# Hybrid mixer layers: gate and up blocks moved among the branch blocks, planner durations and buffer pools changed

## The chip, the core and the metric

The kernel runs on one core of a Trainium2 chip. The metric is the device time of one execution in microseconds; the median of three runs is quoted. "Layer" below is one of the two layers of the model that the kernel computes in one launch.

## What is computed

The input x is one sequence of 256 tokens by 2048 columns. Each of two layers does the following (all in float32):

```
h      = rmsnorm(x)
proj   = h @ w_in                      # 2048 columns in, 35 blocks of columns out
ya     = dilated_window_attention(a_q, a_k, a_v; three groups of four heads) * silu(a_z)
yb     = latent_attention(b_cq, b_ckv, b_kr) * silu(b_z)
yc     = mlstm(c_qk, c_v, c_i, c_f, c_o) * silu(c_z)
yd     = state_space_scan(d_u) with a small gated linear layer * silu(d_z)
up[n]  = y[n] @ w_up[n]                # n = a, b, c, d: 512 -> 2048
merged = sum over n of sigmoid(gate[n] + merge_b[n]) * up[n]
x      = x + merged @ w_out
```

## The kernel before

**Weights.** Every float32 weight is streamed from HBM once, in units of 512 KB (two k-tiles of 128 rows by 512 columns). `Stream.split` (lines 322 to 338) splits each unit into a high part `wh` (ScalarE, a cast) and a low part `wl` (VectorE, a subtraction of two SBUF operands). `Stream.get` (line 340) keeps up to three units split ahead of TensorE and six issued ahead on the queue of SyncE. `block` (line 385) multiplies one block: for each k-tile and each of the two token halves it issues three matmuls of 128x128 by 512 columns (high by high, high by low, low by high). A projection block ("in") of 512 columns has 16 k-tiles, so 96 matmuls and 8 units. An up block has 4 k-tiles, 24 matmuls and 2 units. An output block has 96 again.

**Order of the blocks.** `layer_sequence` (line 265) writes the order out by hand. First come 19 head blocks (cqkr, du, x, cqk, bz, cv, co, cz, aq0, ak0, av0, aq1, ak1, av1, az, aq2, ak2, av2, dz) with four small blocks of branch b between them. Then come the 16 gate blocks, named g + column quarter d (0 to 3) + branch n (0 to 3 for a, b, c, d), with d outside and n in the order b, c, a, d. From the sixth gate on, each gate block is followed by the up block of the gate five places before (`LAG = 5`). The small block "glu" of branch d stands after the fifth gate (`GLU_AT = 4`). Four output blocks o0 to o3 end the layer.

**What a gate and an up block leave for other engines.** The gate block's evacuation is two VectorE operations from PSUM into the tile `gate`, then one tanh on ScalarE. The bias row `mb` is loaded by a DMA on the queue of SyncE at the block's start, into a tile that has one buffer. `merge` (line 1332) follows an up block: two VectorE operations per block, and for all but the first branch of a quarter one GpSimd addition into the accumulator `macc`. The last branch of a quarter spawns `merged` (line 1347), which transposes and splits the sum for the output blocks.

**Branches.** The four branches are Python generators, emitted in small steps between the units of the blocks. Branch d has 16 scan steps of four VectorE products and scans, four GpSimd products and sums (`enter`, `scan`, `leave`, lines 1172 to 1210) with the tables of `d_table` (line 1096); its matmuls are called `dbu` and `dyp`. Branch a (`a_group`, line 676, and `softmax_pv`, line 613) has three groups; its matmuls are `sc`, `pt` and `pv`, and its transposes `tt` and `yt`.

**The planner.** All engine calls go through `Eng` (line 162), whose call stands on line 198; so nearly every instruction shows line 198, and tiles must be read instead. At build time `Plan` (line 107) keeps a clock for each engine from a formula per operation. `tick` (line 364) is called after each unit and emits branch steps in the order e, q, m, b, c, a, d:

```
def can(self, need):
    now = self.clk["PE"] - self.SLACK
    if any(self.ready.get(a.name, (0.0, 0))[0] > now for a in need):
        return False
...
def free(self):
    lim = self.clk["PE"] + self.BACK
    return max(self.clk[e] for e in ("DVE", "ACT", "POOL")) <= lim
...
if not plan.free():
    return
if chains.get(n) and plan.can(need.get(n, ())) and step(n):
```

BACK is 2600 ns. Where a block needs a result that has not been emitted, the rest of that branch is emitted at once: `until("d", ...)` before glu, and `until("abcd"[n], ...)` before an up block. Every engine runs its instructions in the order of emission.

**Pools.** Tiles of 128x1024 come from one pool of `S4B = 28` buffers, tiles of 128x512 from one of `H2B = 12`. A new tile's first writer waits for the last reader of the tile whose buffer it takes; the planner does not know of these waits.

Of the kernel before, what the change touches and what calls it, by code (L numbers as in the profile page):

```python
# [35 lines left out]
LAG = 5  # L36
S4B, H2B, WARM = 28, 12, 8
GLU_AT = 4
# [23 lines left out]
for _d in range(4):  # L62
    for _n in UP_ORDER:
        COLS.append((f"g{_d}{_n}", _rng(GATE + _n * D + _d * 512)))
# [42 lines left out]
class Plan:  # L107
    """Estimates when each engine gets through what has been emitted so far, to choose what to emit next."""
# [4 lines left out]
    def __init__(self, nc):  # L113
        self.nc = nc
        self.clk = dict(PE=0.0, ACT=0.0, DVE=0.0, POOL=0.0, DMA=0.0)
        self.ready, self.used = {}, {}
        self.banks, self.pins = [], set()
        self.sine = False

    LAT = dict(PE=60.0, ACT=140.0, DVE=130.0, POOL=100.0, DMA=100.0)  # L120

    def run(self, eng, cost, outs, ins):
        t = self.clk[eng]
        for a in list(ins) + list(outs):
            r, e = self.ready.get(a, (0.0, eng))
            if e != "PE" or eng != "PE":
                t = max(t, r + self.LAT[e])
        for a in outs:
            u, e = self.used.get(a, (0.0, eng))
            if e != eng:  # L130
                t = max(t, u + self.LAT[e])
        t += cost
        self.clk[eng] = t
        for a in list(outs) + list(ins):
            self.used[a] = (max(t, self.used.get(a, (0.0, eng))[0]), eng)
        for a in outs:
            self.ready[a] = (t, eng)

    def bank(self, tile):
        """The branch bank that a new tile takes: free ones first, then the one that is free soonest."""  # L140
        if len(self.banks) < 4:
            self.banks.append(tile.name)
            return
        free = [b for b in self.banks if b not in self.pins]
        old = min(free, key=lambda b: self.used.get(b, (0.0, 0))[0])
        self.banks[self.banks.index(old)] = tile.name
        self.used[tile.name] = self.used.get(old, (0.0, "PE"))

    def can(self, need):
        """Whether the tensor engine could go on with these tiles and two banks without waiting."""  # L150
        now = self.clk["PE"] - self.SLACK
        if any(self.ready.get(a.name, (0.0, 0))[0] > now for a in need):
            return False
        return 4 - len(self.banks) + sum(b not in self.pins and self.used.get(b, (0.0, 0))[0] <= now
                                         for b in self.banks) >= 2
# [6 lines left out]
class Eng:  # L162
# [3 lines left out]
    def __getattr__(self, name):  # L166
        fn = getattr(self._r, name)
        p, e = self._p, self._e

        def call(*args, **kw):  # L170
            aps = [(k, a) for k, a in list(enumerate(args)) + list(kw.items()) if isinstance(a, bass.AP)]
            outs = [a for k, a in aps if k in (0, "out", "accum_out")]
            ins = [a for k, a in aps if k not in (0, "out", "accum_out")]
            n = max(a.free_size() if callable(a.free_size) else a.free_size for a in (outs if name != "reduce_sum"
                    and name != "reduce_max" else ins))
            psum = any(a.space == bass.MemoryType.PSUM for _, a in aps)
            srcs = [a.space == bass.MemoryType.PSUM for k, a in aps if k not in (0, "out", "accum_out")]
            ptr = any(k in ("scale", "bias", "scalar", "scalar1", "scalar2") or e == "DVE" and isinstance(k, int)
                      and name != "tensor_tensor" and a.free_size() == 1 for k, a in aps)
            if e == "PE":  # L180
                cost = 108.0 if name == "transpose" else 2.3 + (n if kw["lhsT"].dtype == F32R else 4 * max(n, P)) / 2.4
                if aps[0][1].shape[0] <= 32:
                    cost = 122.0 if name == "matmul" else 108.0
            elif e == "ACT":
                cost = 0.833 * n + (52 if any(srcs) else 92) + 93 * (ptr + ("accum_out" in kw))
                f = kw.get("func", args[2] if len(args) > 2 else None)
                if f in (AF.Sin, AF.Exp, AF.Tanh) and (f == AF.Sin) != p.sine:
                    p.sine = not p.sine
                    cost += 1283
            elif e == "POOL":  # L190
                cost = 160 + 0.84 * n if name == "tensor_scalar" else 145 + 2.11 * n
            elif name == "reciprocal":
                cost = 68 + 6.1 * n
            else:
                cost = 68 + n * (0.52 if name in ("tensor_scalar", "tensor_copy", "memset") and not psum else 1.04)
                cost += 62 * ptr
            p.run(e, cost, [a.name for a in outs], [a.name for a in ins])
            return fn(*args, **kw)  # L198

        return call  # L200
# [3 lines left out]
def hybrid_kernel(ctx: ExitStack, tc: tile.TileContext, x_in, pos, win, wup, wout, wuq, wukv, wglu, pp_in, db_in,  # L204
# [60 lines left out]
    def layer_sequence(l):  # L265
        seq = []
        for nm, _ in COLS:
            if nm[0] == "g":
                break
            seq.append(("in", nm))  # L270
            if nm in SMALL:
                seq.append(SMALL[nm])
        gs = [nm for nm, _ in COLS if nm[0] == "g"]
        for i, nm in enumerate(gs):
            seq.append(("in", nm))
            if i == GLU_AT:
                seq.append(("glu", "glu"))
            if i >= LAG:
                seq.append(("up", gs[i - LAG]))
        for i in range(len(gs) - LAG, len(gs)):  # L280
            seq.append(("up", gs[i]))
# [70 lines left out]
    def step(name):  # L352
        """Emit the next part of a chain; it says which tiles the tensor engine reads in the part after."""
# [10 lines left out]
    def tick():  # L364
        """Emit parts of the chains as long as no engine falls behind or waits by the estimate."""
# [19 lines left out]
    def block(key, lhs, K, n):  # L385
        """lhs(k, t) -> (high, low) stationary operands; returns the two accumulators."""
# [27 lines left out]
    def rsqrt(z, E=G):  # L414
        """z <- z ** -0.5 elementwise, z > 0 (bit seed, three Newton steps)."""
# [18 lines left out]
    def frac(dst, src, c, tmp):  # L434
        """dst <- src*c minus its nearest integer."""
# [6 lines left out]
    def turns(ang, shape, parts=4):  # L442
        """ang / (2 pi) modulo 1 as an unevaluated list of terms, largest first; a generator that returns it."""
# [17 lines left out]
    # positions -> rotary tables  # L461
# [30 lines left out]
    def half_angle(r, sin_o, cos_o, t1, t2):  # L492
        """sin and cos of 2 pi r for |r| <= 1/2 (and a little beyond)."""
# [33 lines left out]
    def prep_h(o, d, xb):  # L527
        """xb [P, 2, 512]: columns d*512.. of x; the transposed, scaled, split operand and the squares."""
# [45 lines left out]
    def y_split(o, n, t, y):  # L574
        """y [P tok, 512] of branch n, token half t -> transposed, split."""
# [11 lines left out]
    def silu2(o, ps, name):  # L587
        """(1 + tanh(z/2)) * z/r for z = r*ps, both halves; silu(z) is r/2 times that."""
# [13 lines left out]
    def to_T(src, dst, scale=None, nh=4):  # L602
        """src [P tok, 2, nh*128] -> dst [P, nh, 256], rows scaled."""
# [9 lines left out]
    def softmax_pv(s0, s1, v, rows):  # L613
        """s0 [P,4,128], s1 [P,4,256]: biased scores (overwritten); v [P, 2, 512].  Yields between PE stages;
        rows(t, psum, mx, den) takes the unnormalised output of token half t."""
# [31 lines left out]
    def a_evac(o, ps, gain_scale, key):  # L647
        """rmsnorm over each head's 128 columns (the gain in the transposed copy), times gain_scale."""
# [90 lines left out]
    def b_latent(o, ps, n, npad, gname, key):  # L739
        """rmsnorm of the first n columns, transposed, scaled by the gain and split (two steps)."""  # L740
# [52 lines left out]
    def rope(dst, src, tab, t, n):  # L793
        """src [P, n, 64] -> dst [P, n, 64] rotated by token half t's tables (gains inside)."""
# [114 lines left out]
    def c_if(o, ps):  # L909
        """Input and forget gates, token-major: i + i_b and log_sigmoid(f + f_b)."""  # L910
# [185 lines left out]
    def d_table(o, c):  # L1096
        """cos and sin of theta*t for the four state tiles of chunk c."""
# [17 lines left out]
    def d_params(o):  # L1115
        """Discretised input matrix, transposed per 32-channel group pair; the output matrix."""
# [142 lines left out]
    def d_glu(o, ps):  # L1259
        """Token-major sigmoid of the gate, with the branch's silu."""  # L1260
# [62 lines left out]
    for l in range(depth):  # L1323
# [8 lines left out]
        def merge(nm, ps):  # L1332
# [3 lines left out]
            if first:  # L1336
                acc_t[d] = s4([P, 2, 512], name="macc")
            acc = acc_t[d]
            tmp = acc if first else gt
            for t in range(2):  # L1340
                V.scalar_tensor_tensor(tmp[:, t], gt[:, t], 1.0, ps[t], op0=ALU.add, op1=ALU.mult)
# [137 lines left out]
def _layout(inp):  # L1479
    """Arrays as the program reads them: permuted, padded, repeated; no arithmetic."""  # L1480
# [93 lines left out]
```

## Time and profile before

| what | us |
|---|---|
| median of three runs (2103.89 to 2108.72) | 2104.13 |
| span of the profiled execution | 2101.5 |
| TensorE busy in it | 2072.1 |
| VectorE busy | 1421.2 |
| ScalarE busy | 1035.3 |
| GpSimd busy | 433.7 |

The profiled execution's span is 2.6 us under the median; sums are made against the span. The busy time of TensorE counts overlapping matmuls once, and a matmul of 512 columns shows some 390 ns although the next one starts after 227 ns; so a stall of less than that difference doesn't show as idle time. The chain that ended last, and the number of matmuls in a stretch, tell more. The profile's PE is TensorE (PEld its weight loads), DVE is VectorE, ACT is ScalarE, POOL is GpSimd and SP is SyncE.

In the first layer the blocks start at these times, found by counting matmuls: aq1 286.8, ak1 315.3, av1 342.0, az 367.6, aq2 397.0, ak2 419.2, av2 448.0, dz 471.8, the first gate 501.6, glu 629.1, o0 964.6 us. The first scan step of branch d starts at 304 us and its last matmul `dyp` at 602 us. The second layer begins at 1055.2 us.

### The profile page before, as it was taken

How to read it: one execution, taken by the hardware profiler on the slowest of the kernel's cores; microseconds unless marked ns; L12 is line 12 of the kernel's file. 1: busy time of each engine (PE TensorE's matmuls, PEld its weight loads, DVE VectorE, ACT ScalarE, POOL GpSimd, SP SyncE). 2: the span in 40 equal slices, each digit the busy share in tenths (PEclk: the TensorE clock that was granted, in tenths of full speed). 3: DMA queues.
4: the chain of work that ended last, by engine and by line, in shares of the span. 5: the costliest groups of instructions: out<-in, count | busy, mean ns of one | idle time of the engine just before them, and what ended most of it. 6: DMA issues, size and time to landing. Idle time of an engine off the chain costs nothing.

```text
span 2101.5 us, 26846 instructions
## 1 busy us (share of the span) xinstructions
PE 2072.1 (99%) x9764; PEld 1703.2 (81%) x9764; DVE 1421.2 (68%) x1817; ACT 1035.3 (49%) x1574; POOL 433.7 (21%) x702
## 2 busy tenths in 40 slices
PE   9999999999999999999999999999999999999999
PEld 7888888877778888888878888778787888888887
DVE  5566667978875666667546666898787566566664
ACT  6556455555444444444445654555554444444432
POOL 1730125142320000011043121352422000000110
PEclk9999999999999999999999999999999999999999
DMA  7554444445556666656655544445545666666665
GB/s 261 164 191 153 158 149 153 153 159 176 179 176 202 206 200 203 200 195 215 230 166 171 191 150 150 151 139 162 171 158 188 214 195 207 200 201 200 196 219 171
DMA packets 111011, 384.60 MB, mean 183 GB/s; under 512 B 12320, under 2 KB 13216, under 8 KB 110880
## 3 DMA queue, kind: packets, MB, share of 16 engines
q1 hardware_dynamic: 108576, 378.40, 55.6%
q10 hardware_dynamic: 2304, 4.50, 0.6%
q8 instruction: 76, 1.25, 0.2%
q14 instruction: 55, 0.45, 0.1%
HBM read 378.66 MB, written 4.19 MB: 182 GB/s over the span
## 4 chain that ended last, share of the span: by engine, by line
PE 84%; DVE 9%; POOL 3%; issue 2%; ACT 1%; DMA 1%; SPq 0%; DVEq 0%; ACTq 0%
PE mm L198 76%; DVE dm L198 3%; DVE wl L198 3%; POOL rst L198 1%; DVE dk L198 1%; PE mb L198 1%; PE pv L198 1%; PE dyp L198 1%; DVE dr L198 1%; PE tt L198 1%; POOL cqq L198 1%; ACT wh L198 1%; PE bsc L198 0%; PE dbu L198 0%; PE pt L198 0%
## 5 line engine op out<-in xcount | busy, mean ns | idle before, releaser
L198 DVE TENSOR_TENSOR wl<-raw,wh 128x1024 fp32r<-128x1024 f32 (+1 forms) x694 | 890.0, 1293 | 555.6 <-ACT wh L198 554.5
L198 ACT CAST wh<-raw 128x1024 fp32r<-128x1024 f32 (+1 forms) x694 | 722.8, 1046 | 821.2 <-PE mm L198 702.1
L198 PE MATMUL mm<-wh,hH 128*128 128x512 f32 (+1 forms) x2240 | 877.3, 392 | 0.0
L198 PE MATMUL mm<-wl,hH 128*128 128x512 f32 (+1 forms) x2240 | 867.2, 387 | 5.3 <-DVE wl L198 5.0
L198 PE MATMUL mm<-wh,hL 128*128 128x512 f32 (+1 forms) x2240 | 866.6, 387 | 0.0
L198 PEld LDWEIGHTS mm<-wl,hH 128*128 128x128 f32 x2240 | 422.2, 188 | 91.0 <-DVE wl L198 8.7
L198 PEld LDWEIGHTS mm<-wh,hH 128*128 128x128 f32 x2240 | 422.1, 188 | 89.6 <-issue 3.9
L198 PEld LDWEIGHTS mm<-wh,hL 128*128 128x128 f32 x2240 | 421.6, 188 | 86.2
L198 POOL TENSOR_TENSOR macc<-macc,gate 128x1024 f32<-128x1024 f32 x24 | 62.5, 2605 | 719.9 <-DVE gate L198 532.7
L198 POOL TENSOR_TENSOR dm<-dm,dm 128x256 f32<-128x256 f32 x64 | 70.4, 1120 | 263.1 <-DVE dm L198 263.0
L198 PE MATMUL mm<-wh,mH 128*128 128x512 f32 x256 | 100.0, 391 | 0.0
L198 PE MATMUL mm<-wh,yH 128*128 128x512 f32 x256 | 99.8, 390 | 0.0
L198 PE MATMUL mm<-wh,mL 128*128 128x512 f32 x256 | 99.6, 389 | 0.0
L198 PE MATMUL mm<-wh,yL 128*128 128x512 f32 x256 | 99.6, 389 | 0.0
L198 PE MATMUL mm<-wl,mH 128*128 128x512 f32 x256 | 99.6, 389 | 0.0
L198 PE MATMUL mm<-wl,yH 128*128 128x512 f32 x256 | 99.6, 389 | 0.0
L198 POOL TENSOR_TENSOR dm<-dm,cosT 128x512 f32<-128x512 f32 x32 | 58.1, 1815 | 100.2 <-DVE dm L198 100.0
L198 PEld LDWEIGHTS mm<-wh,mL 128*128 128x128 f32 x256 | 48.1, 188 | 10.0
L198 PEld LDWEIGHTS mm<-wh,yL 128*128 128x128 f32 x256 | 48.0, 188 | 10.0
L198 PEld LDWEIGHTS mm<-wl,yH 128*128 128x128 f32 x256 | 48.1, 188 | 9.9
L198 PEld LDWEIGHTS mm<-wh,yH 128*128 128x128 f32 x256 | 48.1, 188 | 9.9
L198 PEld LDWEIGHTS mm<-wh,mH 128*128 128x128 f32 x256 | 48.1, 188 | 9.8
(352 smaller groups left out, 1724.4 us busy)
## 6 DMA issues: line engine op xcount, KB each, us to landing
raw<-win SPq DMA_DIRECT2D x544, 512.0 KB, 4.1
raw<-wup SPq DMA_DIRECT2D x64, 512.0 KB, 4.2
raw<-wout SPq DMA_DIRECT2D x64, 512.0 KB, 4.1
mb<-mb_in SPq DMA_DIRECT2D x32, 256.0 KB, 4.6
xb<-x_in SPq DMA_DIRECT2D x7, 512.0 KB, 6.2
raw<-wuq SPq DMA_DIRECT2D x6, 512.0 KB, 4.1
raw<-win SPq DMA_DIRECT2D x8, 272.0 KB, 2.9
raw<-wglu SPq DMA_DIRECT2D x4, 512.0 KB, 4.5
```

The costliest lines, as they stand in the source:

```text
L198: return fn(*args, **kw)
```

## The change

1. A new list `SEQ` gives the order. The gates now run with the branch outside and the column quarter inside (all four of b, then c, a, d). One gate block follows each of av0, aq1, ak1, av1, az, aq2, ak2 and av2, eight in all, and an up block follows a gate as soon as more than `LAG = 2` gates are ahead of the ups. glu stands after the 13th gate. From av0 the order is: av0 g01 aq1 g11 ak1 g21 u01 av1 g31 u11 az g02 u21 aq2 g12 u31 ak2 g22 u02 av2 g32 u12 dz g00 u22 g10 u32 g20 u00 g30 u10 g03 glu u20 g13 u30 g23 u03 g33 u13 u23 u33 o0.
2. The accumulator of a quarter is now the tile of its first gate; there is no separate `macc` tile.
3. The planner's durations differ: a 512-column matmul 226.7 ns instead of 215.6, a scan of 256 columns 594 ns instead of 334, small matmuls at least 111 ns. A new function `port` makes VectorE operations with two SBUF operands (and some others) and all GpSimd operations exclude one another in the planner's clock.
4. The pools are 33 and 9 buffers instead of 28 and 12. A scratch area for DMA descriptors is set to 1024 bytes.
5. The order of gate and up weights in HBM follows the new order; their sizes are the same. Comments are removed.

```diff
-LAG = 5
-S4B, H2B, WARM = 28, 12, 8
-GLU_AT = 4
+LAG = 2
+GATE_AFTER = dict(av0=1, aq1=1, ak1=1, av1=1, az=1, aq2=1, ak2=1, av2=1)
+S4B, H2B, WARM = 33, 9, 8
+GLU_AT = 13
...
+GATES = [f"{d}{n}" for n in UP_ORDER for d in range(4)]
...
+def _sequence():
+    seq, g, u = [], 0, 0
+    for nm in HEADS:
+        seq.append(nm)
+        for _ in range(GATE_AFTER.get(nm, 0)):
+            seq.append("g" + GATES[g])
+            g += 1
+            if g - u > LAG:
+                seq.append("u" + GATES[u])
+                u += 1
+    while g < 16:
+        seq.append("g" + GATES[g])
+        g += 1
+        if g == GLU_AT:
+            seq.append("glu")
+        if g - u > LAG:
+            seq.append("u" + GATES[u])
+            u += 1
+    return seq + ["u" + x for x in GATES[u:]]
...
+        self.held = dict(DVE=[], POOL=[])
...
+    def port(self, eng, t, cost):
+
+        other = self.held["POOL" if eng == "DVE" else "DVE"]
+        moved = True
+        while moved:
+            moved = False
+            for a, b in other:
+                if a < t + cost and t < b:
+                    t, moved = b, True
+        mine = self.held[eng]
+        mine.append((t, t + cost))
+        del mine[:-48]
+        return t
...
+        if shared:
+            t = self.port(eng, t, cost)
...
-                cost = 108.0 if name == "transpose" else 2.3 + (n if kw["lhsT"].dtype == F32R else 4 * max(n, P)) / 2.4
+                if name == "transpose":
+                    cost = 109.0
+                elif kw["lhsT"].dtype == F32R:
+                    cost = max(111.0, 13.4 + n / 2.4)
+                else:
+                    cost = 5.0 + 4 * max(n, P) / 2.4
...
+            elif name == "tensor_tensor_scan":
+                cost = 62 + 2.08 * n
...
+            two = sum(a.free_size() > 1 if callable(a.free_size) else a.free_size > 1 for a in ins) > 1
+            shared = name != "memset" and (e == "POOL" or e == "DVE" and not psum and (
+                two or name in ("tensor_scalar", "tensor_copy") and n > 64))
+            p.run(e, cost, [a.name for a in outs], [a.name for a in ins], shared)
...
-                acc_t[d] = s4([P, 2, 512], name="macc")
+                acc_t[d] = gt
             acc = acc_t[d]
-            tmp = acc if first else gt
             for t in range(2):
-                V.scalar_tensor_tensor(tmp[:, t], gt[:, t], 1.0, ps[t], op0=ALU.add, op1=ALU.mult)
+                V.scalar_tensor_tensor(gt[:, t], gt[:, t], 1.0, ps[t], op0=ALU.add, op1=ALU.mult)
...
-    nc = bacc.Bacc("TRN2", target_bir_lowering=False, num_devices=1)
+    nc = bacc.Bacc("TRN2", target_bir_lowering=False, num_devices=1, dynamic_dma_scratch_size=1024)
```

## Rows read from the trace of the kernel before

**Rows 1.** Page, part 1: busy us, share of the span, instructions.

```profile
PE 2072.1 (99%) x9764; PEld 1703.2 (81%) x9764; DVE 1421.2 (68%) x1817; ACT 1035.3 (49%) x1574; POOL 433.7 (21%) x702
```

**Rows 2.** Chain that ended last, two pieces: start us, us, what.

```profile
750.76 108.82 PE mm L198 x480
...
507.33 24.50 PE mm L198 x108
```

**Rows 3.** Stretches: length; busy PE, PEld, DVE, ACT, POOL; clock; DMA; GB/s.

```profile
295.00:620.00 325.00, 317.96 (x1537) 254.98 (x1536) 270.74 (x381) 169.85 (x286) 113.15 (x126) 0.99 0.50 162
500.00:550.00 50.00, 50.00 (x247) 41.33 (x246) 38.77 (x69) 27.65 (x39) 9.31 (x8) 1.00 0.58 186
550.00:600.00 50.00, 46.88 (x211) 35.40 (x210) 45.95 (x49) 18.97 (x19) 27.66 (x18) 0.97 0.48 156
645.00:960.00 315.00, 315.00 (x1403) 261.11 (x1402) 197.13 (x176) 136.02 (x134) 24.82 (x10) 1.00 0.61 199
1290.00:1603.00 313.00, 306.96 (x1525) 247.43 (x1523) 255.41 (x381) 166.39 (x311) 114.85 (x151) 1.00 0.49 158
```

**Rows 4.** PE groups by shape, 295 to 620 us.

```profile
L198 PE MATMUL mm<-wh,hH 128*128 128x512 f32 x394 | 157.1, 399 | 0.0
...
L198 PE MATMUL dyp<-dm,dc 128*32 128x256 f32 x64 | 12.9, 385 | 3.8 <-DVE dm L198 3.8
...
L198 PE MATMUL pv<-av,pT 128*128 128x128 f32 x72 | 8.5, 275 | 0.0
...
L198 PE MATMUL sc<-akT,aqT 128*128 128x256 f32 x24 | 5.9, 382 | 0.0
...
L198 PE MATMUL sc<-akT,aqT 128*128 128x128 f32 x24 | 3.2, 274 | 0.0
...
L198 PE MATMUL dbu<-uH,bbH 32*128 32x256 f32 x32 | 5.4, 328 | 0.0
...
L198 PE MATMUL pt<-ident,as 128*128 128x128 f32 x36 | 4.4, 272 | 0.0
...
L198 PE MATMUL tt<-ident,aqk 128*128 128x128 f32 x32 | 4.4, 275 | 0.5 <-DVE aqk L198 0.5
...
L198 PE MATMUL yt<-ident,aO 128*128 128x128 f32 x8 | 1.0, 272 | 0.0
```

**Rows 5.** Chain, 295 to 425 us: runs of small matmuls.

```profile
296.87 2.62 PE sc L198 x16
...
422.10 0.99 PE dyp L198 x8
...
423.09 0.91 PE dbu L198 x12
...
387.69 1.31 PE pt L198 x12
...
391.77 2.68 PE pv L198 x24
```

**Rows 6.** Chain, 550 to 602 us, share by line.

```profile
by line: DVE dm L198 30.3%; DVE wl L198 15.8%; PE mm L198 12.6%; DMA raw<-win 11.3%; issue 10.2%; PE dyp L198 7.1%; DVE gate L198 5.2%; ACT wh L198 3.6%; PE dbu L198 2.1%; DVE cosT L198 1.3%; SPq L217 0.7%; DVEq L198 0.5%; ACTq L198 0.1%
```

**Rows 7.** DVE and POOL work of a gate block and an up block.

```profile
L198 DVE TENSOR_TENSOR wl<-raw,wh x115: 1209/1225/3349, 647.7 to 958.2; 128x1024 fp32r<-128x1024 f32 x115
...
L198 DVE SCALAR_TENSOR_TENSOR gate<-mm,r,mb x64: 735/744/752, 529.5 to 1976.3; 128x512 f32<-128x512 f32 x64
...
L198 DVE SCALAR_TENSOR_TENSOR gate<-gate,mm x48: 672/680/683, 689.6 to 2010.6; 128x512 f32<-128x512 f32 x48
...
L198 POOL TENSOR_TENSOR macc<-macc,gate x24: 2393/2400/3237, 691.1 to 2011.4; 128x1024 f32<-128x1024 f32 x24
```

**Rows 8.** Scan branch, tile dm: duration ns min/median/max.

```profile
L198 POOL TENSOR_TENSOR dm<-dm,dm x64: 720/1114/2116, 305.7 to 1586.4; 128x256 f32<-128x256 f32 x64
...
L198 DVE TENSOR_TENSOR_SCAN dm<-mag,dm x64: 653/683/1230, 326.5 to 1596.8; 128x256 f32<-128x256 f32 x64
```

**Rows 9.** Timeline, second layer: a transpose run that waited (idle before, releaser).

```profile
1096.54 2.28 PE L198 MATMUL bl<-ident,blat 128*128 128x128 f32 x8 [4.95 <-ACT blat L198]
```

More of the change, by code (lines that the diff above doesn't have):

```diff
@@ L61 @@
 COLS.append(("dz", _rng(D_Z)))
-for _d in range(4):
-    for _n in UP_ORDER:
-        COLS.append((f"g{_d}{_n}", _rng(GATE + _n * D + _d * 512)))
+for _d, _n in [(d, n) for d in range(4) for n in UP_ORDER[:3]] + [(d, UP_ORDER[3]) for d in range(4)]:
+    COLS.append((f"g{_d}{_n}", _rng(GATE + _n * D + _d * 512)))
+HEADS = [nm for nm, _ in COLS if nm[0] != "g"]
+GATES = [f"{d}{n}" for n in UP_ORDER for d in range(4)]
[18 more added lines that the diff above has]
+    return seq + ["u" + x for x in GATES[u:]]
+SEQ = _sequence()
 NCOL = {nm: len(c) for nm, c in COLS}
@@ L118, in __init__, with run @@
         self.sine = False
+        self.held = dict(DVE=[], POOL=[])
     LAT = dict(PE=60.0, ACT=140.0, DVE=130.0, POOL=100.0, DMA=100.0)
-    def run(self, eng, cost, outs, ins):
+    def port(self, eng, t, cost):
[10 more added lines that the diff above has]
+        return t
+    def run(self, eng, cost, outs, ins, shared=False):
         t = self.clk[eng]
@@ L196, in call @@
                 cost += 62 * ptr
-            p.run(e, cost, [a.name for a in outs], [a.name for a in ins])
+            two = sum(a.free_size() > 1 if callable(a.free_size) else a.free_size > 1 for a in ins) > 1
+            shared = name != "memset" and (e == "POOL" or e == "DVE" and not psum and (
+                two or name in ("tensor_scalar", "tensor_copy") and n > 64))
+            p.run(e, cost, [a.name for a in outs], [a.name for a in ins], shared)
             return fn(*args, **kw)
@@ L266, in layer_sequence @@
         seq = []
[L267 to L270, printed above, removed]
+        for nm in SEQ:
+            if nm == "glu":
+                seq.append(("glu", nm))
+            else:
+                seq.append(("up", "g" + nm[1:]) if nm[0] == "u" else ("in", nm))
             if nm in SMALL:
                 seq.append(SMALL[nm])
[L273 to L281, printed above, removed]
         for d in range(4):
```

## The prediction

> **What bounds the kernel now.** The page's busy times come first: TensorE shows 99% of the span [rows 1]. That figure hides stalls, because each matmul of 512 columns is shown for some 390 ns while the next starts sooner. How much sooner is seen in the chain of the gate stretch: 480 of them in 108.82 us, 226.7 ns each, with nothing between them [rows 2]. From 645 to 960 us the kernel is at TensorE's pace and no edit of other engines can shorten it.
>
> The stretch that differs is that of branch d's scan beside branch a, 295 to 620 us. I sum what its matmuls need. There are 1181 of 512 columns (three shapes of 394, 394 and 393, one row of them shown) at 226.7 ns: 267.7 us. The small ones are taken at runs on the chain that had no wait inside [rows 4, 5]: 64 dyp as 8 runs of 0.99 (7.9), 72 pv as 3 of 2.68 (8.0), 48 sc as 3 of 2.62 (7.9), 96 dbu (three shapes of 32) as 8 of 0.91 (7.3), and 76 transposes (pt, tt, yt) at 1.31/12 = 0.109 (8.3). The sum is 307.1 us of 325.0, so TensorE lost 17.9 us here. VectorE is the reason: it is busy 270.74 of 325 us (83%) [rows 3]. Two stretches inside show how the loss depends on its load. From 500 to 550 us VectorE is at 78% and TensorE shows no idle time [rows 3]; half of that stretch is one piece of 108 matmuls in 24.50 us, 226.9 ns each, the full pace [rows 2]. From 550 to 600 us it is at 92%, TensorE is idle 3.1 us outright and the granted clock falls to 0.97, a short fall to the lower of its two levels, 1.2 GHz, which costs 3% of 50 us, 1.5 us [rows 3]. In that stretch the chain lies on VectorE's dm and wl for 46% and on the plain matmuls for 12.6% [rows 6]: the rest of branch d is being emitted at once, ahead of glu. The second layer's stretch, 1290 to 1603 us, has nearly the same load (255 of 313 us, 82%) and TensorE count [rows 3]; I take 17 us of loss there. Both layers together lose about 35 us. A further wait, 4.95 us of TensorE at the latent transposes of the second layer [rows 9], belongs to the start of a layer.
>
> **The change part by part.**
>
> *Matmuls, splits, DMAs.* None is added or removed. A moved gate takes 8 weight DMAs and one of bias rows with it on SyncE's queue, an up block 2; their order among the others is that of the blocks, as before. The bias tile has one buffer, so its DMA waits for the gate before and the weight DMAs queue behind it. Between moved gates now stands a head block, so that wait is over sooner than before. Cost nothing, covered by the weights issued six units ahead.
>
> *Eight gates and their ups before dz, glu eight gates later.* Before glu a layer has eight more gates and ten more ups. TensorE gets 8 x 96 + 10 x 24 = 1008 matmuls, 228.5 us, in the time that branch d may take. VectorE gets per gate 8 splits of 1.225 and 2 evacuations of 0.744, 11.3 us; per up 2 splits and 2 products of 0.680, 3.8 us [rows 7]; together 128.5 us. The stretch to glu becomes 307.1 + 228.5 = 535.6 us of TensorE work against 270.7 + 128.5 = 399.2 us of VectorE, 75%. That is under the 78% at which TensorE had no idle time. It isn't spread evenly, since the planner emits branch d whenever VectorE's clock is not over 2.6 us ahead of TensorE's; the front of the stretch will be above 75% and the rear near the gate stretch's 63% (197 of 315 us) [rows 3]. So I don't take the whole 35 us. Bounds: 0 (VectorE stays full while the scan lasts, and the wait only moves) and 35. I take two thirds, 23 us, nearer to the row of 78% than to that of 92%, because the forced rest of branch d ahead of glu has 230 us more to be done in.
>
> *GpSimd's additions.* Six macc additions a layer now fall into the stretch (ups of c, and the first two of a), 2.40 us each [rows 7], 14.4 us of an engine that is busy 113 of 325 us there. An addition waits for its up block's products, and branch d's sums queue behind it on GpSimd; branch d has slack for that. Cost nothing with that slack; without it at most 14.4 us a layer.
>
> *Planner durations.* A scan was planned at 334 ns and takes 653 to 1230, median 683; it is planned at 594 now [rows 8]. A GpSimd sum of 256 columns is planned at 685 ns in both, takes 720 to 2116, median 1114 [rows 8], and now may be pushed behind VectorE's two-operand work by the new exclusion. So the planner fills VectorE with less work that it can't do in time; that is part of the 23 us. At the start of a layer the same exclusion holds back the GpSimd steps of d's tables, behind which the latent branch waited [rows 9]. No row shows by how much. Bounds: 5 us lost (other steps come late) and 5 us won. I take 2 won, since the planner's error was on the side of too much GpSimd work.
>
> *The end of a layer.* The four sums are now finished by the last four ups. o0 needs the second sum at its start, with u23 and u33 (2 x 24 x 0.227 = 10.9 us) between; the third and fourth are needed four k-tiles ahead of their use, also 10.9 us after their ups. What must fit into that is two products (1.36), an addition (2.40) and eight transposes (0.87) with their split, some 7 us: covered. If that cover were gone, up to 7 us a layer.
>
> *Accumulator in the gate's tile, HBM order, scratch size:* nothing; no instruction changes but its address. *Pools:* below.
>
> **Sum.** 2101.5 - 23 - 2 = 2076.5 us of span. The profiled span stands 2.6 us under the median, so 2079 us.
>
> **The rivals.**
>
> *Deeper.* Nearly all of the 35 us goes, and the waits at the layers' starts with it (5 us). For: the 78% stretch runs without idle time. Against: greedy emission. 2104 - 40 = 2064, from 2054 to 2066. Chance 0.14.
>
> *The wait only moves.* The rule for emission is unchanged: VectorE is kept full until the scan is done, so the scan has the same 83% load for as long as before, and only the forced part ahead of glu goes, 3.1 us of idle time and 1.5 us of clock, some 5 us a layer. For: that leaves 13 of the 17.9 us outside 550 to 600 us. Against: the planned scan is now near the measured one. 2104 - 10 = 2094, from 2091 to 2110. Chance 0.17.
>
> *Slower: nine short buffers.* A step of the scan holds up to eight 128x512 tiles (two of each of two steps, and products of two more), a group of branch a four (the scores and three transposed probabilities). Twelve buffers held both; nine don't. Then a product on VectorE waits until TensorE has read the probabilities, some 7 us from pt to the end of pv (387.69 to 394.45 us) [rows 5], and the splits queue behind it. TensorE has three units of 12 matmuls as a reserve, 8.2 us. The wait decides where it is longer than that with a split of 1.225 us behind it. For: the arithmetic of the buffers. Against: no wait of VectorE on a freed buffer is among the rows before. If each of six groups stops TensorE for 8 us, 48 us are lost against 23 won: 2104 + 25 = 2129, from 2110 on. Chance 0.11.
>
> *Held back too far.* If the planner's exclusion is too strict, branch d isn't finished at glu and its rest is forced again: 2104 - 35 + 2 x 5 = 2079, within the forecast's range. By the Trainium skill's page "SBUF — State Buffer", section "Who interferes with whom", a GpSimd instruction and a VectorE one with two SBUF inputs exclude each other for the whole instruction. The measured scan agrees only at times [rows 8] (median 683 ns beside a minimum of 653), the GpSimd sum mostly (1114 beside 720). By that rule, as an estimate and at most, VectorE would pay for all of the 113 us of GpSimd and the 14 of additions, which brings 399 to 526 of 536 us: full, and this rival would be the likeliest. The rows speak against it, because VectorE's 270.7 us already contain what it waited. I give it 0.06.
>
> **How the numbers follow.** Forecast 2079, own range 2066 to 2091, chance 0.52. Two in ten may be left out: the range runs from 2056 (most of the deeper case) to 2107 (the moved wait). A measurement of this kernel tells 0.3%, 6.3 us, from no change: faster is below 2097.8, slower above 2110.4. Faster: 0.52 + 0.14 + 0.06 + about 0.07 of the moved wait = 0.79. Same: the other 0.10. Slower: 0.11.
>
> **What would show it.** In the changed profile: the chain between av0 and glu on plain matmuls in long pieces; VectorE near 75 to 80% there; no forced run of dyp ahead of glu and no fall of the clock there; dyp spread over more than 300 us; a gate stretch as before at 226.7 ns. It would be wrong if VectorE waits for TensorE's pv or for GpSimd ahead of a dm product (buffers), if the stretch keeps 15 us of loss a layer, or if o0 starts with a wait for macc's successor.

## The result and the profile after

The changed kernel takes 2088.52 us (median of four runs, 2087.09 to 2089.20) against 2104.14 for the kernel before. The ratio is 0.9924, with a 95% interval of 0.9910 to 0.9938: faster by 15.6 us. The forecast was 2079 us with a range from 2056 to 2107. The sign and the range held, but the gain is under two thirds of the 25 us that were forecast, and most of it comes from another place. That the time lies inside the range is in part luck: the term of 23 us came to 3.2, and the one of 2 us to 12.4.

In the kernel after, the helper that records nearly every instruction stands on line 253 (on other lines in the experiments' kernels, such as L225 or L246). First the page's busy times and the shares of the chain that ended last, after:

```profile
PE 2065.0 (99%) x9764; PEld 1702.1 (82%) x9764; DVE 1418.9 (68%) x1817; ACT 1034.8 (50%) x1574; POOL 446.9 (21%) x702
...
PE 95%; DVE 3%; DMA 1%; POOL 1%; ACT 0%; issue 0%; SPq 0%; DVEq 0%; ACTq 0%
```

The same share line of the kernel before:

```profile
PE 84%; DVE 9%; POOL 3%; issue 2%; ACT 1%; DMA 1%; SPq 0%; DVEq 0%; ACTq 0%
```

As in [rows 1], 99% says little. The chain says more: it left TensorE for 16% of the span before and for 5% after. It doesn't say that 11% of the time was won, because the chain runs through VectorE wherever that engine was never waiting, even if TensorE lost only a little there. What TensorE itself waited for stands in the view of its waits (what waited, what ended the wait, us in total, times, longest). Before:

```profile
PE dyp L198 <- DVE dm L198: 5.3, 6, 1.3
PE mm L198 <- DVE wl L198: 5.0, 6, 1.8
PE bl L198 <- ACT blat L198: 5.0, 1, 5.0
PE cg L198 <- POOL gi L198: 3.0, 1, 3.0
PE xt L198 <- DMA xb<-x_in: 3.0, 2, 1.8
```

After:

```profile
PE mm L253 <- DVE aqk L253: 7.9, 2, 5.5
PE mm L253 <- DVE gate L253: 3.9, 1, 3.9
PE mm L253 <- DVE wl L253: 2.6, 4, 1.6
PE xt L253 <- DMA xb<-x_in: 1.5, 1, 1.5
```

The waits of the scan's matmuls (dyp) and the two at the starts of the layers (bl, cg) are gone. Three new ones of 11.8 us stand in their place: a block that can't start because the accumulator banks that it writes still hold the block two places before. They stand at ak1 in the first layer (2.3 us, at 363 us, for the banks of aq1), at the first up block u01 (5.5 us, at 418, for the banks of ak1) and at az in the second layer (3.9 us, at 1514, for the banks of g31). Between the two blocks stands a full gate block in the first two cases (g11, g21) and a short one, the up block u11, only in the third. With each goes a fall of the clock, seen in the stretches (length; busy PE, PEld, DVE, ACT, POOL; clock; DMA; GB/s):

```profile
283.00:860.00 577.00, 567.52 (x2652) 464.03 (x2651) 424.29 (x528) 284.57 (x398) 130.46 (x132) 0.99 0.53 180
340.00:390.00 50.00, 46.05 (x209) 36.33 (x208) 36.04 (x45) 25.87 (x39) 18.35 (x25) 0.97 0.51 169
390.00:440.00 50.00, 44.47 (x200) 35.55 (x199) 38.49 (x50) 21.77 (x36) 17.68 (x24) 0.93 0.45 155
...
1325.00:1894.00 569.00, 563.58 (x2629) 461.22 (x2629) 406.66 (x501) 277.60 (x391) 115.19 (x124) 1.00 0.54 183
1500.00:1530.00 30.00, 25.61 (x123) 21.18 (x122) 20.06 (x28) 13.84 (x30) 6.07 (x4) 0.94 0.40 131
```

The clock's share lost is 3% of 50, 7% of 50 and 6% of 30 us: 6.8 us. The second fall begins before its wait is over:

```profile
412.20:417.70 5.50, 0.02 (x1) 0.00 (x0) 5.43 (x7) 1.04 (x1) 2.47 (x2) 0.84 0.02 9
417.70:423.00 5.30, 5.25 (x13) 4.21 (x14) 2.96 (x4) 0.00 (x0) 0.00 (x0) 0.53 0.51 187
```

So 16% of 5.5 us, 0.9 us, is counted in the wait already. With the 11.8 us of waiting, the new waits cost about 17.7 us.

To see where time went, I cut each span at the first matmul of the block bz and at the first of o0 in each layer, found by counting matmuls in the timeline. The blocks of every cut are the same in all kernels (a little branch work can lie on either side of a cut).

| us | start to bz | bz to o0 | o0 to bz of layer 2 | bz to o0 | o0 to the end | span |
|---|---|---|---|---|---|---|
| before | 99.5 | 865.1 | 184.0 | 860.9 | 92.0 | 2101.5 |
| after | 94.4 | 865.4 | 176.7 | 857.4 | 92.8 | 2086.7 |

Of the 14.8 us between the two spans, 5.1 and 7.3 are from the starts of the two layers, where the order of the blocks did not change. The long stretches in which the gates were moved gave 3.2 us in all (0.3 lost, 3.5 won). Each row is one execution, and its figures move by some 2 us between kernels with the same waits: e6 below, which differs from the kernel after in its pools alone, has 96.9, 863.2, 176.7, 856.7 and 92.8 us. About 1.5 of the 5.1 us is a shorter wait for the first input's DMA (xt: 3.0 us before, 1.5 after, 3.4 in e6); what remains is near the 3.0 us of the cg wait.

### The profile page after: what moved, and what is told of

Its sections match the earlier page's. It is cut to its first block, busy times and chain, and to the rows that moved or that the text cites. A ratio compares the mean times of both kernels' runs of the same rounds, so it can differ in the third digit from the quotient of the medians.

```text
span 2086.7 us, 26821 instructions
## 1 busy us (share of the span) xinstructions
PE 2065.0 (99%) x9764; PEld 1702.1 (82%) x9764; DVE 1418.9 (68%) x1817; ACT 1034.8 (50%) x1574; POOL 446.9 (21%) x702
## 4 chain that ended last, share of the span: by engine, by line
PE 95%; DVE 3%; DMA 1%; POOL 1%; ACT 0%; issue 0%; SPq 0%; DVEq 0%; ACTq 0%
PE mm L253 86%; PE mb L253 2%; PE pv L253 1%; DVE dk L253 1%; PE tt L253 1%; PE dyp L253 1%; PE sc L253 1%; PE dbu L253 1%; DVE wl L253 1%; DVE dm L253 1%; DVE dr L253 1%; PE bsc L253 1%; PE pt L253 1%; DMA raw<-win 0%; PE xt L253 0%
## 5 line engine op out<-in xcount | busy, mean ns | idle before, releaser
L253 DVE TENSOR_TENSOR wl<-raw,wh 128x1024 fp32r<-128x1024 f32 (+1 forms) x694 | 909.0, 1323 | 533.8 <-ACT wh L253 530.8
L253 POOL TENSOR_TENSOR gate<-gate 128x1024 f32<-128x1024 f32 x24 | 62.5, 2603 | 590.9 <-DVE gate L253 590.9
L253 POOL TENSOR_TENSOR dm<-dm,dm 128x256 f32<-128x256 f32 x64 | 76.3, 1213 | 354.9 <-DVE dm L253 345.9
L253 POOL TENSOR_TENSOR dm<-dm,cosT 128x512 f32<-128x512 f32 x32 | 48.9, 1529 | 85.0 <-DVE dm L253 84.9
```

## The experiments

The theory (A): the planner's new durations removed the waits at the layers' starts; the new order removed the scan's waits, but gave their time away to late evacuations of accumulators. The first rival (B): the order alone gave the gain. A further one came up with the first runs (C): the durations are right but need time ahead of glu, and the moved gates are only one way to provide it. Ratios are to the kernel before, measured in the same session, with 95% intervals.

### Was the scan forced ahead of glu? (e3)

```diff
-GLU_AT = 4
+GLU_AT = 7
```

> The kernel of before with glu three gates later and nothing else. If the dyp waits (14 us in both layers, with a fall of the clock) come from the forced rest of the scan ahead of glu, they go: 2088 to 2096 us. If VectorE's load by itself makes them, they stay: 2100 to 2106 us.

Measured: 2104.65 us, ratio 0.9995 (0.9986 to 1.0004): no change. The waits of TensorE:

```profile
PE dyp L198 <- DVE dm L198: 6.4, 6, 2.2
PE mm L198 <- DVE wl L198: 5.0, 6, 1.8
```

glu now starts at 708.7 us instead of 629.1, yet the first layer's three longest dyp waits stand at 575.9, 577.3 and 596.2 us, in the same blocks (g00 and g03) as before (572.8, 574.2 and 593.1). So nothing was forced there. The prediction's reading of [rows 6] was wrong: the planner had itself emitted these steps too early, and TensorE's dyp stood in its queue before their operands were there. It is tempting to blame the scan, planned at half of its measured duration. In the new order that isn't the cause: e7 below has the longer scan and dyp waits of 9.4 us, e11 has the old one with the exclusion and none.

### The durations alone and the order alone (e1, e2)

e1 is the kernel before with `Plan` and `Eng` of the kernel after, its scratch size, and pools of 31 and 12 buffers:

```diff
-S4B, H2B, WARM = 28, 12, 8
+S4B, H2B, WARM = 31, 12, 8
...
+            elif name == "tensor_tensor_scan":
+                cost = 62 + 2.08 * n
...
+        if shared:
+            t = self.port(eng, t, cost)
```

> The order of before with the planner durations of after (pools 31 and 12, since 28 and 12 cannot be allocated with them). Theory A (the durations removed the waits at the two layer starts, some 12 us, and the new order gave almost nothing because its gain went into new waits for accumulator banks): 2088 to 2096 us, with no wait of TensorE over 1 us on cg or bl in the first 100 us of a layer. Theory B (the order gave the gain, through the longer time that the scan has ahead of glu): 2100 to 2110 us, with the waits at the layer starts still there.

e2 is the kernel after with `Plan` and `Eng` of the kernel before:

```diff
-            elif name == "tensor_tensor_scan":
-                cost = 62 + 2.08 * n
...
-        if shared:
-            t = self.port(eng, t, cost)
```

> The order and the pools of after with the planner durations of before. Theory A: the waits at the layer starts (3.2 us on cg, 5.1 us on bl) stay, the forced dyp waits ahead of glu go; 2090 to 2100 us, and the waits for accumulator banks are absent or smaller, if it is the stricter durations that emit the evacuations late. Theory B: 2085 to 2092 us, all of the gain.

Measured: e1 2151.29 us, ratio 1.0210 (1.0196 to 1.0224); e2 2140.38 us, ratio 1.0160 (1.0146 to 1.0174). Each half alone is slower than the kernel before, by 45 and 34 us, and together they are faster. Neither theory had foreseen that. TensorE's waits in e1:

```profile
PE dyp L225 <- DVE dm L225: 37.7, 20, 5.9
PE mb L225 <- ACT dgH L225: 15.8, 2, 7.9
```

and two stretches of e1's first layer, while the scan is planned and where glu stands:

```profile
400.00:600.00 200.00, 200.00 (x966) 164.41 (x965) 146.19 (x219) 106.70 (x169) 40.77 (x55) 1.00 0.56 178
605.00:670.00 65.00, 29.88 (x98) 12.84 (x99) 49.04 (x62) 10.72 (x10) 32.07 (x26) 0.58 0.13 44
```

From 400 to 600 us VectorE is at 73% and TensorE never stops: with the new durations the planner no longer overfills VectorE. But the scan is slower for that. At glu the rest of it is emitted at once, TensorE is busy for 30 of 65 us, and the clock's mean is 0.58. That is the rival "held back too far", in a pure form: it takes place when the time ahead of glu is not there. The waits on cg and bl are gone (o0 to bz of layer 2 takes 175.8 us as after, 176.7), with the order of before: so that part is due to the durations.

TensorE's waits in e2:

```profile
PE mm L226 <- DVE wl L226: 14.8, 5, 5.7
PE dyp L226 <- DVE dm L226: 14.2, 10, 3.8
PE bl L226 <- ACT blat L226: 4.9, 1, 4.9
PE mm L226 <- DVE gate L226: 4.8, 1, 4.8
...
PE cg L226 <- POOL gi L226: 3.2, 2, 3.0
```

Splits (wl) and scan steps (dm) both come late. The reading that the moved gates bring more VectorE work into a stretch in which the planner, with the old durations, already plans too much is argued from the order. The waits at the layers' starts stay. Theory A's part on the starts is shown; B falls.

### Time ahead of glu without moving the gates (e5, e8)

e5 is e1 with the pools of the kernel after and glu three gates later; e8 is e1 with glu three gates later and the edit of e4 (below).

```diff
-GLU_AT = 4
+GLU_AT = 7
...
-S4B, H2B, WARM = 31, 12, 8
+S4B, H2B, WARM = 33, 9, 8
```

> The order of before with the planner durations and the pools (33 and 9) of after, and glu three gates later (GLU_AT 7). In e1 four of the eight dyp groups of the first layer and two of the second were left for the forced part at glu. Theory C (the durations are right and need time ahead of glu; the moved gates are one way to give it): three more gates with their ups, some 82 us, leave at most one group to be forced: 2085 to 2098 us. If the place of the gates among the branch blocks is what matters, the forced part stays: 2130 to 2150 us.

> As e5 with pools 31 and 12, and the evacuations emitted after half of the next block as in e4. Theory C with theory A: the scan ends near glu and no accumulator bank is waited for: 2072 to 2090 us. If the old order lacks time for the scan: over 2100 us.

Measured: e5 2097.18 us, ratio 0.9956 (0.9944 to 0.9969), 54 us faster than e1; e8 2100.29 us, 0.9971 (0.9960 to 0.9983), which is where it was expected if the old order lacks time for the scan. e5's waits:

```profile
PE dyp L225 <- DVE dm L225: 8.7, 5, 3.4
PE mb L225 <- ACT dgH L225: 7.9, 1, 7.9
PE mm L225 <- DVE wl L225: 4.1, 4, 1.8
```

What is left is a last forced part of the scan in the first layer, at 690 to 720 us; e8 has it too (clock 0.72 in those 30 us). In the second layer, where the scan starts earlier, nothing is forced, and bz to o0 takes 852.5 us, 4.9 less than in the kernel after. So C holds in its main part: what the moved gates buy is time. That all of the new durations are right is taken back by e11 below. In this order no accumulator is waited for, and so the earlier evacuation of e8 had nothing to remove.

### The pools and the planner's exclusion (e6, e7, e11)

e6 changes the pools of the kernel after; e7 is e6 without the exclusion.

```diff
-S4B, H2B, WARM = 33, 9, 8
+S4B, H2B, WARM = 31, 12, 8
```

> The kernel of after with pools of 31 and 12 buffers instead of 33 and 9. If nine short buffers cost waits (the slower rival), it is faster: 2075 to 2085 us. Theory A (nothing waits for them): the same, 2085 to 2092 us, with the same waits for accumulator banks.

```diff
-        if shared:
-            t = self.port(eng, t, cost)
```

> The kernel of after with pools 31 and 12 and without the planner's exclusion of VectorE and GpSimd; the other new durations stay. If the exclusion is what keeps VectorE from being overfilled and what holds d's tables back at a layer's start: 2105 to 2135 us, with dyp and wl waits as in e2 and the bl wait back. If the scan's longer duration does it: 2080 to 2095 us.

Measured: e6 2087.85 us, ratio 0.9910 (0.9895 to 0.9925), with the same three waits (7.9 and 3.9 us). Nine short buffers cost nothing. e7 2145.53 us, ratio 1.0182 (1.0168 to 1.0196), 57.7 us slower than e6 and slower than either expectation. Its waits:

```profile
PE mm L251 <- DVE wl L251: 17.8, 7, 4.9
PE bl L251 <- ACT blat L251: 10.9, 3, 8.6
PE dyp L251 <- DVE dm L251: 9.4, 8, 2.6
```

Of the 54.8 us between the two spans, 34.7 are in the long stretches (880.5 and 874.1 us from bz to o0) and 19.8 at the layers' starts (109.2 and 184.2 us). The longer scan alone removes neither the late splits and scan steps nor the wait of bl. e11 is the counterpart: the kernel after, with the exclusion, and the durations of matmuls and scan of before.

```diff
-                if name == "transpose":
-                    cost = 109.0
-                elif kw["lhsT"].dtype == F32R:
-                    cost = max(111.0, 13.4 + n / 2.4)
...
+                cost = 108.0 if name == "transpose" else 2.3 + (n if kw["lhsT"].dtype == F32R else 4 * max(n, P)) / 2.4
...
-            elif name == "tensor_tensor_scan":
-                cost = 62 + 2.08 * n
```

> The kernel of after with the planner's exclusion kept and the durations of matmuls and scan as in before. With e7 this splits the planner's part. If the exclusion is nearly all of it: 2084 to 2096 us. If the scan's duration (334 ns planned, 683 measured) matters as well: 2100 to 2125 us, with dyp waits back.

Measured: 2077.54 us, ratio 0.9868 (0.9853 to 0.9883): faster than the kernel after by 11 us, better than its range. The longest waits:

```profile
PE xt L246 <- DMA xb<-x_in: 2.5, 2, 1.3
PE mm L246 <- DVE gate L246: 2.3, 1, 2.3
PE mm L246 <- DVE aqk L246: 1.9, 2, 1.5
PE cg L246 <- POOL gi L246: 1.5, 1, 1.5
```

The starts of the layers take 96.5 and 176.2 us, so the exclusion is also what shortened them (cg is left with 1.5 us). It is the part of the new durations that matters, and the corrected matmul and scan durations, though nearer to the rows, cost 11 us beside it: the waits on accumulators are 4.2 us here and 11.8 in the kernel after.

### Why accumulators are evacuated late (e4, e12, e9, e10)

The longest new wait, before the first up block, in the timeline of the kernel after (start us, us, engine, line, operation):

```profile
410.86 0.90 POOL L253 TENSOR_SCALAR ass<-ass,r 128x4 f32<-128x4 f32 x2
...
411.14 0.49 DVE L253 SCALAR_TENSOR_TENSOR dk<-cc,dhi,dk 128x256 f32<-128x256 f32 x1
...
411.72 1.55 POOL L253 TENSOR_TENSOR dm<-dm,cosT 128x512 f32<-128x512 f32 x1
...
412.06 1.49 DVE L253 SCALAR_TENSOR_TENSOR dk<-cc,dhi,dk 128x256 f32<-128x256 f32 x1
...
413.23 1.44 POOL L253 TENSOR_TENSOR dn<-dm,dr 128x512 f32<-128x512 f32 x1
413.59 1.36 DVE L253 SCALAR_TENSOR_TENSOR dr<-cc,dlo,dk 128x256 f32<-128x256 f32 x1
...
416.93 1.28 DVE L253 TENSOR_TENSOR aqk<-mm,ass 128x512 f32<-128x512 f32 x2
417.72 0.29 PEld L253 LDWEIGHTS mm<-wh,yH 128*128 128x128 f32 x1 [5.92 <-issue]
417.75 0.77 PE L253 MATMUL mm<-wh,yH 128*128 128x512 f32 x1 [5.53 <-DVE aqk L253]
```

The scale factors (ass) are there at 411.8 us. The evacuation (aqk) that needs them runs at 416.9, behind table steps of branch d and a split that were emitted before it. VectorE is not overloaded in the 50 us around it (77%), though in the wait itself it works without a pause (5.43 of 5.5 us); the order in its queue is what costs. Two of the table steps there take 1.49 and 1.36 us instead of 0.49: each began while a GpSimd operation (dm, dn) was running, which adds some 1.9 us. The remaining evacuation steps (chain "e") are emitted at once at the end of the next block, just before the block that needs the banks.

e4 emits them after half of the next block, e9 the same only for blocks of branch a, gates and ups, e10 after a quarter; e12 leaves the place and exempts chain "e" from the planner's limit:

```diff
             tick()
-        if not small:
-            drain("e")
+            if not small and k >= K // 2:
+                drain("e")
...
+            if key[2][0] in "ag" and k >= K // 2:
...
+            if key[2][0] in "ag" and k >= K // 4:
...
-                if not plan.free():
+                if n != "e" and not plan.free():
```

> The kernel of after; the remaining evacuation steps of a block are emitted after half of the next block instead of at its end. Theory A: the three long waits of TensorE for accumulator banks (2.5, 5.7 and 4.1 us on aqk and gate) and the clock falls behind them (6.8 us) go: 2070 to 2080 us. If VectorE is simply too far behind there, the waits only change their name (wl, dm): 2085 to 2092 us.

> As e4 (remaining evacuation steps emitted after half of the next block), but only during blocks of branch a, gate and up blocks; the first head blocks are as in after. e4 had a new wl wait of 3.0 us and a cg wait of 1.1 us in the first 180 us, with a fall of the clock. If those come from the early evacuation of the first head blocks: 2074 to 2079 us. If not: 2080 to 2082 us as e4.

> As e9 with the remaining evacuation steps emitted after a quarter of the next block. If an accumulator bank is still waited for in e9 (1.0 us on gate in e4), this takes it away: up to 2 us faster than e9. If steps emitted too early make VectorE and ScalarE wait for GpSimd's chain of small operations in front of the splits, it is 2 to 10 us slower than e9.

> The kernel of after, where the evacuation steps alone are exempt from the planner's limit of 2.6 us. If that limit is what emits the aqk evacuations late: the waits for accumulator banks go, 2072 to 2082 us. If it is the planner's readiness test (the sum of squares not ready by its clock), they stay: 2085 to 2092 us.

| | us | ratio (95%) | bz to o0, both layers |
|---|---|---|---|
| e4 | 2080.67 | 0.9876 (0.9863 to 0.9890) | 858.2, 854.7 |
| e9 | 2074.60 | 0.9856 (0.9839 to 0.9872) | 852.8, 853.7 |
| e10 | 2088.53 | 0.9923 (0.9908 to 0.9938) | 859.6, 860.8 |
| e12 | 2079.40 | 0.9879 (0.9864 to 0.9894) | 853.5, 857.1 |

e4 has a new wl wait of 2.9 us at 170 us, among the first head blocks, with a fall of the clock; in e9, which leaves those blocks as they were, it is gone. e9's waits, and its stretch of the moved gates:

```profile
PE mm L253 <- DVE wl L253: 2.6, 4, 1.0
...
PE mm L253 <- DVE gate L253: 0.8, 1, 0.8
```

```profile
280.00:860.00 580.00, 578.28 (x2725) 474.78 (x2723) 433.96 (x542) 292.70 (x407) 122.05 (x133) 1.00 0.56 185
```

The aqk waits are gone, one gate wait of 0.8 us is left, and the clock is at 1.00 throughout. VectorE has the same share of work in that stretch as after (75% and 74%): no work was taken away, only its order changed. e9 is faster than both kernels, 14 us ahead of the kernel after. e12 says what delays the evacuations: without the planner's 2.6 us limit the two aqk waits go as well. Its gate wait stays:

```profile
PE mm L253 <- DVE gate L253: 3.9, 1, 3.9
```

A gate's evacuation is emitted right behind its block and not as a step of chain "e", so the limit can't delay it; what stands ahead of it on VectorE does. e10 shows the other side:

```profile
PE mm L253 <- DVE wl L253: 12.6, 9, 2.1
PE mm L253 <- DVE gate L253: 1.8, 1, 1.8
```

Emitted after a quarter, the steps reach the queues ahead of splits, and nine waits for wl of 12.6 us take the place of what was removed; 14 us more than e9 was beyond the 2 to 10 expected. The rows show how: ahead of the three longest (1.9, 2.1 and 2.0 us, at 356, 1444 and 1611 us) VectorE stood waiting for GpSimd's scale factors (ass) for 3.8, 4.9 and 3.8 us with the splits behind it. The first of them:

```profile
353.74 1.29 DVE L253 TENSOR_TENSOR aqk<-mm,ass 128x512 f32<-128x512 f32 x2 [3.80 <-POOL ass L253]
354.94 3.48 DVE L253 TENSOR_TENSOR wl<-raw,wh 128x1024 fp32r<-128x1024 f32 x3
```

VectorE waits so in e9 too (34.1 us in 11 waits, 46.7 in 12 in e10, 4.5 in 5 in the kernel after), but there TensorE's waits for wl stay at 2.6 us.

## Why the prediction was right or wrong

**What bounds the kernel: right.** The scan's stretch is where TensorE lost time [rows 3, 4], and the gate stretch stayed at its pace. The loss of 17.9 us in the first layer is about right: e9 wins 12.3 us there. The 17 of the second layer were taken by likeness, and no run won more than 9.4 us there (e11, 851.5 us).

**"The rest of branch d is being emitted at once, ahead of glu": wrong.** e3 moved glu by 80 us and the waits stayed where they were. The same step carried the choice of two thirds ("because the forced rest of branch d ahead of glu has 230 us more to be done in"). The time ahead of glu does matter, but for the other reason: with the new durations the scan takes longer, and without the time it is forced (e1, e5).

**Eight gates and their ups, 23 us: mis-sized.** The load was right: 75% was worked out, 424 of 577 us (74%) and 407 of 569 (71%) were measured. The dyp waits went, as forecast. But the two stretches gave 3.2 us (6.1 in e6), because "the wait only moves" took place in another form than the rival had: not VectorE's load, but the order in its queue, about 17.7 us with the clock. Where that is mended, in e9, the same two stretches give 12.3 and 7.2 us against the kernel before, 19.5 in all. The term was about the right size for what order and durations together make possible, and the change gives most of it back. What was missed is that a block's accumulator banks are needed again two blocks on; a wait for them was not in the list of costs at all. For the gate wait (3.9 us) the step from a full block to a short one fits: an up block lasts 5.4 us, so that the banks of the block before it are needed again 5.4 us after that block's end. For the two aqk waits (7.9 us) it does not, since a full block of 21.8 us stood in between; there the planner's limit left the steps to the end of that block (e12). Of the signs that the prediction named, there is no forced run of dyp, but dyp is spread over 286 and 289 us, not over 300 (242 and 263 before), and the clock does fall.

**Planner durations: place right, size wrong.** "I take 2 won" at the layers' starts, with 5 as a bound: 5.1 and 7.3 us were won, of which about 1.5 us is the input's DMA: beyond the bound still. The bound was taken from one wait of 4.95 us [rows 9]; it left out the cg wait of the first layer (3.0 us) and the fall of the clock behind the bl wait. Within the long stretches, too, the exclusion is decisive (34.7 us between e6 and e7), where the prediction only said that it is "part of the 23".

**The exclusion rule.** The Trainium skill's page "SBUF — State Buffer", section "Who interferes with whom", says that a GpSimd instruction that reads SBUF and a VectorE one with two SBUF inputs shut each other out for the whole instruction. The scan's row after the change (656 ns at least, median 681, at most 1228) is as in [rows 8]; most scans are not held up. The prediction took that as agreement "only at times" and as evidence against planning by the rule. The traces agree with the rule more often than that: of the 64 scans in the kernel after, 20 take 1.15 to 1.23 us, and each of these was started while a GpSimd operation was running and ends 0.55 us after it; the 44 others take at most 0.69. In the kernel before it is 27 of 64 (0.92 to 1.23 us, all of this kind); one scan there took 0.68 us although GpSimd was at work throughout. The median hides this, because most scans meet no GpSimd operation. The runs show that the plan is better with the rule. Whether the rule or simply the more cautious clocks do it was not separated.

**Slower, nine short buffers: refuted** by e6, as the prediction's "no wait of VectorE on a freed buffer" had suggested. **Held back too far:** not in the kernel after, but e1 shows its price, 45 us over the kernel before, well above what the prediction gave it. **Deeper:** not reached by this change; e9 comes to within 11 us of its 2064.

**The end of a layer: right.** o0 to the end took 92.8 us against 92.0, with no wait among those of TensorE.

**Open.** Why the corrected matmul and scan durations make the evacuations later (after against e11) was not isolated. It fits e12 that more time charged to VectorE makes the 2.6 us limit bind more often. Removing the limit together with e9 or e11's durations was not tried. Nor was the old order with the exclusion alone, or with glu later than e5 has it: whether gates have to be moved among the branch blocks at all, or a later glu would do, is open.

## What to carry to other kernels

When an order written at build time uses estimated durations, the estimates and the slack ahead of a deadline are one change: here each alone cost 34 to 45 us, and both together won 16. When the order of blocks changes, follow the accumulator banks: what must be evacuated before the next block but one, how much time a short block in between leaves for it, and what stands ahead of that evacuation in its engine's queue. A busy share that is right doesn't settle it; the gain of 14 us between the kernel after and e9 came at an equal VectorE load.

## What was unexpected of the hardware

Waits of TensorE of 2.3 us (until 363 us), 5.5 us (until 418) and 3.9 us (until 1514) each came with a fall to the lower clock level: the granted clock is 0.97, 0.93 and 0.94 in the stretches that hold them. The clock adds about 5.9 us to 11.8 us of waiting, so that in this trace a wait of a few us costs about one and a half times its length. It isn't certain for a short wait: e6 has the same first wait, 2.3 us until 366 us, and there the clock stays at 1.00:

```profile
360.00:370.00 10.00, 7.67 (x35) 6.03 (x34) 6.90 (x10) 4.11 (x4) 7.96 (x15) 1.00 0.52 156
```

In e9, where no wait in that stretch is over 1.0 us, the clock stays at 1.00.

In these traces the length of a scan goes by whether a GpSimd operation is under way when it starts: in the kernel after 20 of 64 take 1.15 to 1.23 us and end 0.55 us after that operation, and none of the others takes over 0.69 us. The two table steps of 1.49 and 1.36 us in the timeline above are of the same kind.
